# The beginning of a trunk kernel: inputs through two queues, squares in more buffers, the last square summed by its own matmuls, a first power taken early, and low weight halves made by adding transfers

## The chip, the core and the metric

The kernel runs on one core of one Trainium2 chip. A core has engines that run side by side, each with its own instruction stream in order: TensorE (PE, matrix products; its weight loads are shown as PEld), VectorE (DVE, elementwise), ScalarE (ACT, functions of one input), GpSimd (POOL) and SyncE (SP, which issues transfers). Transfers (DMAs) run on 16 DMA engines that all issuing queues share. The metric is the device time in microseconds, the median over runs.

## The reference

A trunk of two layers on 512 positions of width 1024: one layer with a gated linear recurrence (HGRN2), one with chunked band attention, each with a gated FFN behind it. The change lies in the first sub-layer, of which this is the part that matters:

```python
c_act = jax.nn.silu(c)
sm = jax.nn.softmax(a_lb.astype(jnp.float32), axis=0)
lower_bounds = jnp.cumsum(sm, axis=0) - sm[0]
...
mod = c_act @ mod_w[layer] + mod_b[layer]
sh1, sc1, g1, sh2, sc2, g2 = jnp.split(mod, N_MOD, axis=-1)
u = modulate(rms_norm(h, norm_mix[layer]), sh1, sc1)
...
q, z_f, v, g = jnp.split(u @ w_in, [A_FORGET_DIM, 2 * A_FORGET_DIM, 2 * A_FORGET_DIM + D_MODEL], axis=-1)
q = jax.nn.silu(q)
sig = jax.nn.sigmoid(zf)
f = lbf + (1 - lbf) * sig
```

`rms_norm(x, gain)` is `x * rsqrt(mean(x * x) + 1e-6) * gain`, and `modulate(x, shift, scale)` is `x * (1 + scale) + shift`. `v` are the values of the recurrence; `lbf` are the lower bounds of its forget gate.

## The kernel before

Everything is kept transposed: a tile is 128 features (partitions) by 512 positions, and eight tiles `h[0]` to `h[7]` hold the residual stream. Products are made in three passes, because PE takes the operands in a rounded 32-bit format (F32R): each operand is split into a high part (a rounded copy, made by ACT) and a low part (the difference, made by DVE), and `mm3` (L180) adds high x high, high x low and low x high. A weight block of 128 x 1024 is loaded into a buffer `raw` (three of them), `split` (L120) makes `wh` on ACT (L123) and `wl` on DVE (L128). For one pair of FFN blocks per layer, which `by_transfer` (L116) names, `wl` is made in another way: ACT writes the negated rounded copy (L125) and POOL issues a transfer that adds `raw` to it (L126). `fetch` (L147) splits one block ahead of its use, and one more where the next is by transfer.

The start runs in this order:

- SP loads `cols` (all column vectors), `ident`, the eight `h`, and then in turn rows of the modulation matrix (`mrow`, 512 KB) and first weight blocks (`fall`, `first_r`, 384 KB).
- ACT loads the table of its sigmoid and makes `csig`; DVE makes `cact` = silu(c), and eight scaled identities `dc` from it, which PE multiplies by ones (L955) to spread `cact` over all partitions; ACT copies that to `crow`. ACT also loads the table of Exp for the lower bounds (L99 to L108).
- The mean square: ACT squares each `h[j]` (L223, L227, two buffers), DVE adds the squares up in `acc` (L230), PE sums over partitions with four one-column matmuls (`mean_square`, L235). `rstd` (L238) adds epsilon on ACT (L242) and raises to -0.5 on POOL (L244), which is the first power in the kernel. `bcast` (L247) makes four scaled identities `dg` on DVE and spreads them by PE into `rb`.
- For each j, `mod_entry` (L615) makes one column of the modulation by a 128 x 1024 multiply and sum on DVE (L618), `prepare` (L633) makes the modulated tile `u_t` (L641), its high part `u00h` on ACT (L645) and its low part `u00l` on DVE (L648), and `low` (L630) the low part of the first weights; `first_mm` (L662) then runs 18 products into six banks. The sixth and seventh tile take the shift too (`shifted`, L655), and their parts are called `u0h` and `u0l` (L658, L659); the other six get theirs behind the first products, in `complete`.
- Between those, PE runs matmuls whose results are never read (L959 and L967, into `first[0]`, which the first product overwrites); they keep PE occupied.
- Next come the values, `value_half(0)`: four blocks `av_0_0` to `av_0_3`, each used by 24 matmuls (L206 to L208). Around them `evacuate` copies the six banks (L1002) and `shift_sums` (L993, L995) sums shift products, which PE sums once more at L1025. The gates follow, from L686, and need `lb` and `oml` at L702 to L707.

The order in this stretch is written out by hand (`tc.manual_schedule()`); behind it, a scheduler orders what the generators yield. All engines work in order: an instruction that waits holds up everything behind it on its engine, and SP's loads, which wait for free buffers, do so too.

## Time and profile before

| | us |
|---|---|
| median of 3 runs | 1282.65 |
| the runs | 1279.99, 1282.65, 1286.14 |
| the profiled execution | 1283.68 |
| its span, first to last instruction | 1281.5 |
| first product that counts starts at | 19.09 |
| values' products start at | 53.67 |

A row of the timeline has the start, the duration, the engine, the line, the operation and the tiles (out<-in); numbers of buffers are left out, so `av_l` is any `av_0_k_l`. In brackets stands how long the engine sat idle before, and what ended that. A row of a table of waits has the total, the count and the longest, in us. PE's matmuls are pipelined, so two in sequence may overlap in the rows.

### The profile page before, as it was taken

To read this page: it belongs to the slowest core of one execution; us is meant where nothing else is said; L and a number is where in the kernel's file an instruction comes from. 1 tells how busy PE (TensorE), PEld (TensorE's weight loads), DVE (VectorE), ACT (ScalarE), POOL (GpSimd) and SP (SyncE) were. 2 spreads that over 40 slices of the span, in tenths; PEclk is the share of its full clock that TensorE was granted. 3 is DMA by queue.
4 is the path that set the end of the run, shared out by engine and by line. 5 is a ranking of instruction groups with operands and counts; after the bars stand their busy time and mean duration, and the time that the engine had idled before them with its cause. 6 is when DMAs were issued, how large, how long until landed. Compare 5 with 4: busy or idle time off the path is not lost.

```text
span 1281.5 us, 21575 instructions
## 1 busy us (share of the span) xinstructions
PE 1255.6 (98%) x8544; PEld 1070.2 (84%) x8544; DVE 990.7 (77%) x1812; ACT 637.7 (50%) x1119; POOL 20.8 (2%) x28
## 2 busy tenths in 40 slices
PE   7999999999999999999999999999999999999996
PEld 6878778788899999978888766676889999998886
DVE  7998888946999999986359656776798888884324
ACT  4464436443655565642228456674465556563220
POOL 0000000000000000000000000000000000000000
PEclk9999999999999999999999999999999999999999
DMA  9456666522455655666342322211333333342321
GB/s 367 166 181 194 224 223 207 193 80 85 109 203 182 197 185 195 209 204 204 91 130 82 107 74 73 79 58 34 115 91 107 104 114 113 100 124 91 94 88 66
DMA packets 53333, 177.55 MB, mean 139 GB/s; under 512 B 6000, under 2 KB 9456, under 8 KB 53232
## 3 DMA queue, kind: packets, MB, share of 16 engines
q1 hardware_dynamic: 52656, 174.08, 41.3%
q0 software_dynamic: 576, 2.10, 1.0%
q8 instruction: 67, 1.10, 0.4%
q14 instruction: 34, 0.28, 0.1%
HBM read 171.96 MB, written 2.10 MB: 136 GB/s over the span
## 4 chain that ended last, share of the span: by engine, by line
PE 81%; DVE 12%; DMA 3%; issue 2%; ACT 1%; POOL 1%; SPq 0%; POOLq 0%; DVEq 0%; ACTq 0%
PE f_r L532 8%; PE f_r L533 8%; PE f_r L531 7%; PE f_o L185 6%; PE f_o L183 6%; PE f_o L184 6%; DVE mw L315 2%; DMA mw<-in_modw 2%; PE t L1183 2%; PE f L183 2%; PE f L184 2%; PE f L185 2%; PE s L1166 2%; DVE f_w_l L497 1%; PE bo L1197 1%
## 5 line engine op out<-in xcount | busy, mean ns | idle before, releaser
L532 PE MATMUL f_r<-f_l,f_w_h 128*128 128x256 f32 x1008 | 287.0, 285 | 0.0
L533 PE MATMUL f_r<-f_h,f_w_l 128*128 128x256 f32 x1008 | 282.1, 280 | 0.9 <-DVE f_w_l L497 0.8
L531 PE MATMUL f_r<-f_h,f_w_h 128*128 128x256 f32 x1008 | 280.7, 279 | 0.0
L533 PEld LDWEIGHTS f_r<-f_h,f_w_l 128*128 128x128 f32 x1008 | 189.0, 188 | 2.1 <-DVE f_w_l L497 1.9
L531 PEld LDWEIGHTS f_r<-f_h,f_w_h 128*128 128x128 f32 x1008 | 189.5, 188 | 0.3 <-ACT f_pu L553 0.2
L532 PEld LDWEIGHTS f_r<-f_l,f_w_h 128*128 128x128 f32 x1008 | 189.5, 188 | 0.1
L185 PE MATMUL f_o<-f_p,f_o_l 128*128 128x512 f32 (+1 forms) x374 | 141.6, 380 | 0.5 <-DVE f_o_l L128 0.5
L183 PE MATMUL f_o<-f_p,f_o_h 128*128 128x512 f32 (+1 forms) x374 | 141.9, 380 | 0.0
L184 PE MATMUL f_o<-f_p,f_o_h 128*128 128x512 f32 (+1 forms) x374 | 140.9, 377 | 0.2 <-DVE f_p L448 0.2
L315 DVE SCALAR_TENSOR_TENSOR mw<-mw,crow 128x1024 f32<-128x1024 f32 x96 | 116.8, 1221 | 17.5 <-DMA mw<-in_modw 17.3
L123 ACT ACTIVATE f_o_h<-r_f_o 128x1024 fp32r<-128x1024 f32 (+1 forms) x48 | 46.8, 987 | 137.8 <-PE f_o L184 116.6
L128 DVE TENSOR_TENSOR f_o_l<-r_f_o,f_o_h 128x1024 fp32r<-128x1024 f32 (+1 forms) x48 | 54.0, 1134 | 69.0 <-ACT f_o_h L123 62.4
L496 ACT ACTIVATE f_w_h<-f_x 128x1024 fp32r<-128x1024 f32 x72 | 76.5, 1062 | 49.3 <-PE f_r L532 40.6
L497 DVE TENSOR_TENSOR f_w_l<-f_x,f_w_h 128x1024 fp32r<-128x1024 f32 x72 | 88.0, 1223 | 5.7 <-ACT f_w_h L496 3.2
L496 ACT ACTIVATE f_w_h<-r_f_c 128x1024 fp32r<-128x1024 f32 x72 | 61.0, 847 | 49.0 <-PE f_r L532 47.4
L185 PEld LDWEIGHTS f_o<-f_p,f_o_l 128*128 128x128 f32 x374 | 70.1, 188 | 15.8 <-DVE f_o_l L128 1.9
L184 PEld LDWEIGHTS f_o<-f_p,f_o_h 128*128 128x128 f32 x374 | 70.2, 188 | 14.5 <-DVE f_p L448 0.7
L183 PEld LDWEIGHTS f_o<-f_p,f_o_h 128*128 128x128 f32 x374 | 70.3, 188 | 12.5
L497 DVE TENSOR_TENSOR f_w_l<-r_f_c,f_w_h 128x1024 fp32r<-128x1024 f32 x72 | 68.8, 955 | 10.1 <-ACT f_w_h L496 10.1
L1172 ACT ACTIVATE sb<-sb,st 128x128 f32<-128x128 f32 (+1 forms) x64 | 35.6, 557 | 41.5 <-DVE st L1171 41.3
L1169 DVE CUSTOM_DVE_ANT_0 sb<-s,wb 128x128 f32<-128x128 f32 (+1 forms) x64 | 31.0, 490 | 29.5 <-PE s L1166 29.2
L184 PE MATMUL f<-f_l,f_h 128*128 128x512 f32 x96 | 37.4, 396 | 0.0
(381 smaller groups left out, 2724.2 us busy)
## 6 DMA issues: line engine op xcount, KB each, us to landing
mw<-in_modw SPq DMA_DIRECT2D x96, 512.0 KB, 4.1
r_f_c<-in_ffn_in SPq DMA_DIRECT2D x72, 512.0 KB, 3.4
r_f_o<-in_ffn_out SPq DMA_DIRECT2D x32, 512.0 KB, 3.7
mrow<-in_modw SPq DMA_DIRECT2D x16, 512.0 KB, 8.7
r_f<-in_ffn_in SPq DMA_DIRECT2D x16, 512.0 KB, 3.3
r_f_o<-in_ffn_out SPq DMA_DIRECT2D x16, 384.0 KB, 3.3
r_av<-in_a_v SPq DMA_DIRECT2D x8, 512.0 KB, 3.7
r_g<-in_a_g SPq DMA_DIRECT2D x8, 512.0 KB, 4.5
```

Source lines behind the costliest of these rows:

```text
L123: A.activation(wh, raw, AF.Copy)
L128: V.tensor_sub(wl, raw, wh)
L183: T.matmul(ps, wh[:, kt, :], uh, start=start, stop=False)
L184: T.matmul(ps, wh[:, kt, :], ul, start=False, stop=False)
L185: T.matmul(ps, wl[:, kt, :], uh, start=False, stop=stop)
L315: V.scalar_tensor_tensor(mw, mw, 1.0, crow, op0=ALU.mult, op1=ALU.mult, accum_out=raw[:, j:j + 1])
L496: A.activation(wh, raw, AF.Copy)
L497: V.tensor_sub(wl, raw, wh)
L531: T.matmul(ps, wh[:, j, :], uh, start=f, stop=False, skip_group_check=True)
L532: T.matmul(ps, wh[:, j, :], ul, start=False, stop=False, skip_group_check=True)
L533: T.matmul(ps, wl[:, j, :], uh, start=False, stop=stop and j == 3, skip_group_check=True)
L1172: A.activation(s[:, 0:n], s[:, 0:n], AF.Exp, bias=st[:, 1:2], accum_out=st[:, 2:3])
```

## The change

- `cols`, `ident`, `h3` and `h5` are loaded by transfers that ACT issues; SP issues the other six `h`.
- POOL takes a power of ones early, into `pow0`, which nothing reads.
- The lower bounds move into `bounds()`, called behind the third group of the values' products.
- The low parts of all four blocks of the first half of the values are made by an adding transfer.
- PE's filler matmuls on `h[j]` as they land become three on `h[0]` before the sums, three after and three after the broadcast.
- The squares take three kinds of buffer in turn, two of each; DVE no longer adds the last one to `acc`, and PE sums it with four matmuls of its own, into four more columns. The two copies of `crow` move from ACT into DVE's additions. Epsilon and the two sums are added on DVE.

```diff
--- before.py
+++ after.py
@@ -54,7 +54,7 @@
 V1_AFTER, CREDIT, RATES = 1, 3.0, (3.5, 16, 2.0, 56, 1.5)
 
 
-KEEP = 3
+IDLE = (3, 3, 3)
 
 
 EARLY = (3, 5)
@@ -78,12 +78,13 @@
 
 
     cols = cst.tile([P, NCOL], F32, tag="cols", name="cols")
-    nc.sync.dma_start(cols, d["cols"])
+    A.dma_start(cols, d["cols"])
     ident = cst.tile([P, P], F32, tag="ident", name="ident")
-    nc.sync.dma_start(ident, d["ident"])
+    A.dma_start(ident, d["ident"])
+
     h = [cst.tile([P, S], F32, tag=f"h{j}", name=f"h{j}") for j in range(KT)]
     for j in range(KT):
-        nc.sync.dma_start(h[j], d["xT"][j * P:(j + 1) * P, :])
+        (A if j in (3, 5) else nc.sync).dma_start(h[j], d["xT"][j * P:(j + 1) * P, :])
 
     ones = cst.tile([P, P], F32, tag="ones", name="ones")
     V.memset(ones, 1.0)
@@ -93,19 +94,23 @@
     V.memset(eps, EPS)
     nhalf = cst.tile([P, 8], F32, tag="nhalf", name="nhalf")
     V.memset(nhalf, -0.5)
-
+    pow0 = sm.tile([P, NB], F32, tag="rs", name="pow0")
+    G.tensor_tensor(pow0, ones[:, 0:NB], nhalf[:, 0:NB], op=ALU.pow)
     lb = cst.tile([P, AH], F32, tag="lb", name="lb")
     oml = cst.tile([P, AH], F32, tag="oml", name="oml")
-    lbt = sm.tile([P, AH], F32, tag="lbt", name="lbt")
-    V.tensor_sub(lbt, cols[:, C_LB:C_LB + AH], cols[:, C_LB:C_LB + AH])
-    lbe = sm.tile([P, AH], F32, tag="lbe", name="lbe")
-    A.activation(lbe, lbt, AF.Exp)
-    lbr = sm.tile([P, AH], F32, tag="lbr", name="lbr")
-    V.reciprocal(lbr, lbe)
-    lbs = sm.tile([P, AH], F32, tag="lbs", name="lbs")
-    V.tensor_mul(lbs, lbe, lbr)
-    V.tensor_sub(lb, lbs, lbs)
-    V.tensor_scalar(oml, lb, -1.0, 1.0, op0=ALU.mult, op1=ALU.add)
+
+    def bounds():
+
+        lbt = sm.tile([P, AH], F32, tag="lbt", name="lbt")
+        V.tensor_sub(lbt, cols[:, C_LB:C_LB + AH], cols[:, C_LB:C_LB + AH])
+        lbe = sm.tile([P, AH], F32, tag="lbe", name="lbe")
+        A.activation(lbe, lbt, AF.Exp)
+        lbr = sm.tile([P, AH], F32, tag="lbr", name="lbr")
+        V.reciprocal(lbr, lbe)
+        lbs = sm.tile([P, AH], F32, tag="lbs", name="lbs")
+        V.tensor_mul(lbs, lbe, lbr)
+        V.tensor_sub(lb, lbs, lbs)
+        V.tensor_scalar(oml, lb, -1.0, 1.0, op0=ALU.mult, op1=ALU.add)
 
     cact = cst.tile([P, KT], F32, tag="cact", name="cact")
     csig = sm.tile([P, KT], F32, tag="csig", name="csig")
@@ -115,7 +120,7 @@
 
     def by_transfer(key):
 
-        return key[0] in [f"f{layer}" for layer in FAST] and key[1] == PLAIN - 1
+        return key[0] in [f"f{layer}" for layer in FAST] and key[1] == PLAIN - 1 or key[0] == "av" and key[1] == 0
 
     def split(raw, nk, n, nm, tag, key):
         wh = wp.tile([P, nk, n], F32R, tag=tag + "h", name=f"{nm}_h")
@@ -946,6 +951,11 @@
             load_first(j)
         load_mod(0, 0)
 
+        def idle(n):
+
+            for _ in range(n):
+                T.matmul(first[0][:, 0:256], ones, h[0][:, 0:256], start=True, stop=True)
+
         pcs = []
         for r in range(2):
             dc = hp.tile([P, NB, P], F32, tag=f"on{6 + r}", name=f"dc{r}")
@@ -955,19 +965,35 @@
                 T.matmul(pcs[r][:, k * P:(k + 1) * P], ones, dc[:, k, :], start=True, stop=True)
         gb = cst.tile([P, KT], F32, tag="gb", name="gb")
         V.scalar_tensor_tensor(gb, cols[:, C_MB + 8:C_MB + 16], 1.0, cols[:, C_NM:C_NM + KT], op0=ALU.add, op1=ALU.mult)
+        idle(IDLE[0])
+
+        sqs = []
         for j in range(KT):
-            T.matmul(first[0][:, 0:256], ones, h[j][:, 0:256], start=True, stop=True)
-            square_into(acc, j, "n0")
-        for r in range(2):
-            A.activation(crow[:, r * S:(r + 1) * S], pcs[r], AF.Copy)
-        pst = mean_square(acc, "n0")
+            sq = sm.tile([P, S], F32, tag=("sq", "et", "ut")[j % 3], name=f"n0_sq{j}", bufs=2) if j else acc
+            A.activation(sq, h[j], AF.Square)
+            sqs.append(sq)
+            if 0 < j < KT - 1:
+                V.tensor_add(acc, acc, sq)
+            if j == 3:
+                V.tensor_copy(crow[:, 0:S], pcs[0])
+            elif j == 5:
+                V.tensor_copy(crow[:, S:D], pcs[1])
+        pst = bank("n0_ss")
+        for i, sq in enumerate((acc, sqs[-1])):
+            for b in range(NB):
+                T.matmul(pst[:, NB * i + b:NB * i + b + 1], sq[:, b * P:(b + 1) * P], mean_col, start=True, stop=True)
         a0 = mod_entry(0, 1)
         high(0)
-        for _ in range(KEEP):
-            T.matmul(first[0][:, 0:256], ones, h[0][:, 0:256], start=True, stop=True)
-        rs = rstd(pst, "n0")
+        idle(IDLE[1])
+        ms = sm.tile([P, NB], F32, tag="ms", name="n0_ms")
+        V.tensor_scalar_add(ms, pst[:, 0:NB], EPS)
+        ms2 = sm.tile([P, NB], F32, tag="ms", name="n0_ms2")
+        V.tensor_add(ms2, pst[:, NB:2 * NB], ms)
+        rs = sm.tile([P, NB], F32, tag="rs", name="n0_rs")
+        G.tensor_tensor(rs, ms2, nhalf[:, 0:NB], op=ALU.pow)
         low(0)
         rb = bcast(rs, "n0")
+        idle(IDLE[2])
         prepare(0, a0)
         for j in range(KT):
             if j + 1 < KT:
@@ -1010,6 +1036,8 @@
             evacuate(i)
         for k in range(KT):
             push(4 * k + 1)
+            if k == 2:
+                bounds()
             if k == 0:
                 evacuate(4)
                 evacuate(5)
```

The start on ACT (`csig` is the sigmoid of c, `n0_sq` the squares, `first0_h` the first weights' high part). Before:

```order
L112 ACT_TABLE_LOAD
L112 ACTIVATE csig_108<-cols_67 128x8
L102 ACT_TABLE_LOAD
L102 ACTIVATE lbe_99<-lbt_97 128x8
L223 ACTIVATE acc0_118<-h0_71 128x512
L227 ACTIVATE n0_sq1_0_196<-h1_72 128x512
```

ACT's first rows now:

```order
L81 DMA cols_67<-in_cols 128x177
L83 DMA ident_69<-in_ident 128x128
L87 DMA h3_74<-in_xT 128x512
L87 DMA h5_76<-in_xT 128x512
L117 ACT_TABLE_LOAD
L117 ACTIVATE csig_100<-cols_67 128x8
L973 ACTIVATE acc0_110<-h0_71 128x512
```

Four transfers stand ahead of the first table load, and the second table load with `lbe` has left this place.

PE at the same place (`n0_ss` are the sums over partitions, `n0_rb0` is the broadcast, `first0<-h` are fillers). Before:

```order
L959 MATMUL first0_119<-h5_76,ones_87 128x256
L959 MATMUL first0_119<-h6_77,ones_87 128x256
L959 MATMUL first0_119<-h7_78,ones_87 128x256
L235 MATMUL n0_ss0_225<-mean_89,acc0_118 128x1 x4
L967 MATMUL first0_119<-h0_71,ones_87 128x256 x3
L254 MATMUL n0_rb0_246<-n0_dg0_245,ones_87 128x128 x4
```

And now:

```order
L957 MATMUL first0_111<-h0_71,ones_87 128x256 x3
L984 MATMUL n0_ss_211<-mean_89,acc0_110 128x1 x4
L984 MATMUL n0_ss_211<-mean_89,n0_sq7_209 128x1 x4
L957 MATMUL first0_111<-h0_71,ones_87 128x256 x3
L259 MATMUL n0_rb0_238<-n0_dg0_237,ones_87 128x128 x4
L957 MATMUL first0_111<-h0_71,ones_87 128x256 x3
L188 MATMUL first0_111<-u00h0_252,first0_h_224 128x512
```

The sums are eight matmuls instead of four, and three fillers stand between the broadcast and the first product.

The second place is the step from the first products to the values. ACT before (`u0h` are high parts of the modulated tiles, `f0` and `qq0` take the first products' banks):

```order
L658 ACTIVATE u0h7_479<-u0_t7_472,a0_7_476 128x512
L658 ACTIVATE u0h0_514<-u0_t0_255,a0_0_504 128x512
L123 ACTIVATE av_0_0_h_522<-r_av_0_0_311 128x1024
L658 ACTIVATE u0h1_548<-u0_t1_268,a0_1_512 128x512
L1002 ACTIVATE f0_507<-first0_119 128x512
L1002 ACTIVATE qq0_506<-first1_120 128x512
```

ACT now:

```order
L663 ACTIVATE u0h7_474<-u0_t7_467,a0_7_471 128x512
L663 ACTIVATE u0h0_509<-u0_t0_250,a0_0_499 128x512
L128 ACTIVATE av_0_0_h_517<-r_av_0_0_306 128x1024
L130 ACTIVATE av_0_0_l_518<-r_av_0_0_306 128x1024
L128 ACTIVATE av_0_1_h_522<-r_av_0_1_513 128x1024
L130 ACTIVATE av_0_1_l_523<-r_av_0_1_513 128x1024
L663 ACTIVATE u0h1_549<-u0_t1_263,a0_1_507 128x512
L1028 ACTIVATE f0_502<-first0_111 128x512
```

Three operations on weights have come in between the first block's high part and `u0h1`.

PE there, with what each row waits for (a name that begins with DMASW is the landing of a transfer issued by POOL). Before:

```order
L185 MATMUL first4_123<-u0h7_479,first7_l_470 128x512
L183 MATMUL first5_124<-u0h7_479,first7_h_469 128x512
L184 MATMUL first5_124<-u0l7_480,first7_h_469 128x512
L185 MATMUL first5_124<-u0h7_479,first7_l_470 128x512
L206 MATMUL av_0_0_556<-av_0_0_h_522,u0h0_514 128x512 [waits Activation_49]
L207 MATMUL av_0_0_556<-av_0_0_l_523,u0h0_514 128x512 [waits DVE_49]
L208 MATMUL av_0_0_556<-av_0_0_h_522,u0l0_515 128x512
```

And now:

```order
L190 MATMUL first5_116<-u0h7_474,first7_l_465 128x512
L211 MATMUL av_0_0_557<-av_0_0_h_517,u0h0_509 128x512 [waits Activation_49]
L212 MATMUL av_0_0_557<-av_0_0_l_518,u0h0_509 128x512 [waits DMASW0_49]
L213 MATMUL av_0_0_557<-av_0_0_h_517,u0l0_510 128x512 [waits DVE_49]
L211 MATMUL av_0_1_558<-av_0_0_h_517,u0h0_509 128x512 [waits PE_49]
```

The order of PE is the same; its second matmul of the values now waits for the transfer instead of for DVE. Behind this stretch, the rows of DVE and SP differ by places of one or two, since the scheduler sets them anew.

## The prediction

> **What bounds the kernel now.** I read the page's busy times and its chain of waits first, then the table of what TensorE (PE) waited for, and then the timeline, engine by engine, up to 85 us.
>
> ```profile
> span 1281.5 us, 21575 instructions
> ...
> PE 1255.6 (98%) x8544; PEld 1070.2 (84%) x8544; DVE 990.7 (77%) x1812; ACT 637.7 (50%) x1119; POOL 20.8 (2%) x28
> ...
> PE 81%; DVE 12%; DMA 3%; issue 2%; ACT 1%; POOL 1%; SPq 0%; POOLq 0%; DVEq 0%; ACTq 0%
> ```
>
> PE is busy for 1255.6 of 1281.5 us, and the change removes no matmul that computes a product. It can only let PE start its real work earlier, or make it wait later. Where PE waits:
>
> ```profile
> PE crow L955 <- DVE dc L954: 3.5, 1, 3.5
> ...
> PE first L183 <- ACT u00h L645: 1.5, 1, 1.5
> ...
> PE av L208 <- DVE u0l L659: 0.5, 1, 0.5
> ...
> PE fine L757 <- DVE ks L733: 2.4, 4, 0.8
> PE ot L850 <- DVE oe L841: 1.6, 1, 1.6
> ```
>
> The columns are total, times and longest, in us. The first two lie in the first 19 us. The third is the only wait between 23 and 130 us. The last two, with 1.2 us of smaller ones, make 5.2 us between 130 and 260 us. So the start is a chain that ends at the first product, and from there PE hardly stops. What counts is when that chain ends, and whether PE still finds every operand behind it.
>
> The chain in rows of the timeline (start, duration, engine, line, tiles):
>
> ```profile
> 0.73 1.28 ACT L112 ACT_TABLE_LOAD   x1 [0.73 <-PEq L1442]
> ...
> 1.66 3.75 SPq L86 DMA_DIRECT2D h<-in_xT  x8
> 2.74 0.21 ACT L112 ACTIVATE csig<-cols 128x8 f32<-128x8 f32 x1 [0.72 <-DMA cols<-in_cols]
> ...
> 3.18 1.46 DVE L954 TENSOR_SCALAR dc<-ident,cact 128x128 f32<-128x128 f32 x7
> ...
> 6.22 0.69 DVE L230 TENSOR_TENSOR acc<-acc,n_sq 128x512 f32<-128x512 f32 x1 [0.83 <-ACT n_sq L227]
> ...
> 8.07 4.67 DVE L230 TENSOR_TENSOR acc<-acc,n_sq 128x512 f32<-128x512 f32 x6 [1.16 <-ACT n_sq L227]
> ...
> 12.80 1.05 PE L235 MATMUL n_ss<-mean,acc 128*128 128x1 f32 x8 [1.15 <-DVE acc L230]
> ...
> 14.23 1.82 POOL L244 TENSOR_TENSOR n_rs<-n_ms,nhalf 128x4 f32<-128x4 f32 x1 [13.19 <-ACT n_ms L242]
> ...
> 16.09 0.88 DVE L253 TENSOR_SCALAR n_dg<-ident,n_rs 128x128 f32<-128x128 f32 x4 [0.91 <-POOL n_rs L244]
> ...
> 19.09 0.69 PE L183 MATMUL first<-u00h,first_h 128*128 128x512 f32 x1 [1.50 <-ACT u00h L645]
> ...
> 23.05 0.39 PE L183 MATMUL first<-u00h,first_h 128*128 128x512 f32 x1
> ```
>
> The reader is to see seven dependent additions on DVE that end at 12.74, the sums over partitions on PE, one power of 1.82 us on POOL, and the first product at 19.09.
>
> **The start.** *Loads issued by ACT.* SP issues one load in about 0.46 us (eight in 3.75 us). At that price four take 1.9 us on ACT: the table load moves from 0.73 to 2.6, csig from 2.74 to 3.9, and the eight dc (0.21 us apart) end near 6.1. The trace has no load issued by ACT. If they cost nothing csig stays where it is; at twice SP's price it comes 3 us late. I take SP's price, the same instruction on another queue. SP's own later loads move up by those four issues. *Additions.* The first then stands at 6.2, as before. The second waited 1.16 us for its square, which waited for a load. The first load of h is now issued at 0.73 instead of 1.66 and squares have buffers enough, so I let the additions follow each other 0.80 us apart (six in 4.67 us).
>
> ```profile
> L244 POOL TENSOR_TENSOR n_rs<-n_ms,nhalf x6: 695/1008/1817, 14.2 to 1273.1; 128x4 f32<-128x4 f32 x4, 128x2 f32<-128x2 f32 x2
> ...
> L1190 DVE COPY pt<-t 128x384 f32<-128x384 f32 x16 | 8.9, 555 | 1.2 <-PE t L1183 0.8
> ```
>
> The two copies of crow come from ACT to DVE. One of 384 columns takes 0.56 us, so one of 512 about 0.7; between two dependent additions it also fills their 0.1 us pause and lengthens the row by some 0.45. Six additions and two copies end at 6.2 + 5 x 0.80 + 2 x 0.45 + 0.7 = 11.8, against 12.74. *Sums.* Leaving the last square out of the chain saves an addition but costs four matmuls, eight more PE entries at 1.05 us for eight: PE is through at 11.86 + 2.05 = 13.9, where it was through at 13.85. Two small DVE operations (0.17 us for 128x8 ones, the nearest) replace ACT's bias; the power starts at 14.4, 0.2 us late. *Power.* 1.82 us is the longest of six, the median is 1.0. With pow0 paying the first cost while POOL idles, 0.8 us goes, and the dg start at 15.46 instead of 16.09. **DVE's chain is 0.6 us earlier**; between 0 (the power still costs 1.8) and 1.6 (ACT issues for nothing).
>
> *Fillers.* After its gaps PE ran at half clock:
>
> ```profile
> 15.00:20.00 5.00, 2.29 (x12) 1.34 (x11) 2.74 (x8) 1.36 (x2) 1.05 (x1) 0.92 1.03 417
> 20.00:25.00 5.00, 5.00 (x17) 4.01 (x18) 4.86 (x10) 1.37 (x2) 0.00 (x0) 0.74 1.03 418
> ```
>
> The third column from the right is the granted clock: 0.92 and 0.74 make 3.4 us at half speed, in which eight products came 0.43 us apart and not 0.23, a loss of 1.6 us. Three times three fillers now leave gaps of 2 us at most, so I expect full speed at the first product; if the clock drops all the same, little changes, because PE cannot use most of that gain. DVE feeds it, and at the last of the first products PE has nearly caught up with DVE:
>
> ```profile
> 48.69 0.74 DVE L659 SCALAR_TENSOR_TENSOR u0l<-u_t,a,u0h 128x512 fp32r<-128x512 f32 x1
> ...
> 49.82 0.39 PE L184 MATMUL first<-u0l,first_h 128*128 128x512 f32 x1
> ```
>
> u0l is ready at 49.43 and used at 49.82. With DVE 0.6 earlier PE gets it at 48.8: **PE ends the first products 1.0 us earlier** (0.6 + 0.4), at 52.7 instead of 53.67.
>
> **The values' low parts.** Before, ACT makes the high part, DVE subtracts, and PE uses the result at once:
>
> ```profile
> 50.80 0.73 ACT L658 ACTIVATE u0h<-u_t,a 128x512 fp32r<-128x512 f32 x1 [2.18 <-DVE a L623]
> ...
> 51.44 1.04 ACT L123 ACTIVATE av_h<-r_av 128x1024 fp32r<-128x1024 f32 x1
> ...
> 52.38 0.71 ACT L658 ACTIVATE u0h<-u_t,a 128x512 fp32r<-128x512 f32 x1
> ...
> 52.69 1.22 DVE L128 TENSOR_TENSOR av_l<-r_av,av_h 128x1024 fp32r<-128x1024 f32 x1
> ...
> 53.96 0.50 PE L207 MATMUL av<-av_l,u0h 128*128 128x512 f32 x1
> ...
> 65.88 0.50 PE L208 MATMUL av<-av_h,u0l 128*128 128x512 f32 x1 [0.50 <-DVE u0l L659]
> ```
>
> The subtraction ends at 53.9, its reader runs at 53.96: there is no slack. After, ACT writes a second copy and POOL issues a transfer that adds to it. The same pair stands in this trace for one ffn block:
>
> ```profile
> 344.18 1.04 ACT L125 ACTIVATE f_l<-r_f 128x1024 fp32r<-128x1024 f32 x1
> ...
> 345.54 0.86 POOL L126 DMA_DIRECT2D f_l<-r_f  x1 [2.44 <-ACT f_l L125]
> ...
> L126 POOL DMA_DIRECT2D f_l<-r_f x4: 862/892/1047, 342.0 to 955.6; - x4
> ...
> DMA to landing us min/median/max: 4.6/5.0/5.5
> ```
>
> 1.04 us of ACT, 0.3 us to POOL's start, 5.0 us to the landing. There it is hidden, since that block is split one piece ahead. Here the first piece's copy stands directly behind the high part on ACT: it runs from 52.38 - 0.6 to 52.8, the transfer starts at 53.1 and lands at 58.1. PE's second matmul of the values, due at 53.0, waits 5.1 us, and everything on PE stands behind it. The bounds for the landing are 3.5 us (the page's plain load of r_av, the same 512 KB) and 8.7 us (its mrow, loaded while the queues were full); I take the median of the operation itself. The other three pieces are needed some 5.5 us apart and land in time. ACT's u0h of the next block now stands behind three more weight operations, but PE waits longer than they take. Each raw buffer is held until its transfer has read it, so SP issues the fourth r_av at 58 instead of 53.93, landing near 62; ACT needs it at 65.
>
> *Clock.* The half-speed spell followed gaps of 1.17 and 1.5 us; a stop of 5 us should bring it again, for 1.6 us as above. The Trainium skill, page "TensorE: Matmul & The Clock Gate", section "What's actually happening", says that the clock falls after at least one idle window of about 3.4 us and that windows run freely; read strictly, a 5 us stop need not hold a whole idle window, and the sum would be 1.6 us lower. This trace disagrees: shorter gaps were enough.
>
> *DVE and bounds.* DVE loses four subtractions (4.9 us). Five small operations of bounds, the Exp and its table load (1.28 us) move to about 67 us. There lbe stands on ACT behind the fourth piece's two copies, whose buffer PE frees late, and u0l stands behind it on DVE: I expect PE to wait about 0.6 us there, as much as the wait at 65.88 that goes. DVE's lighter load may take a little of the later 5.2 us of waits; I count 0.5.
>
> **Sum.** The profiled execution took 1283.68 us for its span of 1281.5; it lies 1.03 above the median of 1282.65. -1.0 (start) + 5.1 (stop) + 1.6 (clock) - 0.5 (later) = +5.2: 1288.9 on that execution, **1288 us** on the median.
>
> **Rivals.** *Slow landing* (the other side, clearly slower): at 50 to 55 us the DMA engines are 85% busy, and the transfer reads two operands.
>
> ```profile
> 50.00:55.00 5.00, 5.00 (x23) 3.88 (x22) 4.93 (x10) 4.20 (x8) 0.00 (x0) 1.00 0.85 308
> ```
>
> At a landing of 6.5 us or with a second half-clock spell the loss is 5.2 + 1.5 to 3 = +7 to +8.5: 1290 to 1291.5. It decides from a landing of 6.2 us on. Against it: the four in the trace also ran beside loads. *Absorbed*: DVE's 4.9 us let PE skip the waits between 130 and 260 us, +0 to +2: 1283 to 1285. For it speaks that DVE ends the longest of them; against it that what feeds DVE there (first_b, the scores) comes from PE, and is late with it. *No half clock*, as the page read strictly: 1286.3. *The stop doesn't come* (the change does as its words say, and the low parts are in time): start -1.0 to -2, and the wait of 0.5 goes: 1280 to 1281.5. It needs a landing in under 1 us, against 4.6 at least.
>
> **Chances.** Forecast (1287 to 1289.5) 0.40; slow landing 0.25; no half clock 0.15; absorbed 0.13; no stop 0.07. A measurement of this kernel tells about 0.5% from no change, 6.4 us: slower needs over 1289.1, which takes the slow landing and a sixth of the forecast, 0.31; faster needs under 1276.2, which no case gives, 0.03 for what I have not seen; the rest 0.66. The range 1281.5 to 1292 leaves out the last case and the end of the slow one.
>
> **What would show it.** Right: the dg of the first norm near 15.5, its power near 1.0 us; PE's first product near 18.4 at clock 1.00; "PE av <- DMA" as the longest wait, about 5 us near 53; clock under 0.85 between 55 and 65. Wrong: no such wait; a first product later than 19.1 (ACT's issues dearer than taken); or the waits between 130 and 260 us gone.

## The result and the profile after

The changed kernel takes 1293.01 us (median of four runs, 1291.54 to 1294.31) against 1283.28 for the kernel before (median of four runs, the three above among them): ratio 1.0076, 95% interval 1.0048 to 1.0105. It is slower by about 10 us, where 5.2 were forecast. Its profiled execution took 1294.11 us, with a span of 1292.3.

The page of the changed kernel, busy times and the shares of the chain that ended last:

```profile
span 1292.3 us, 21598 instructions
...
PE 1260.0 (98%) x8548; PEld 1072.3 (83%) x8548; DVE 986.8 (76%) x1811; ACT 639.4 (49%) x1120; POOL 25.5 (2%) x33
...
PE 74%; DVE 13%; DMA 6%; issue 4%; ACT 3%; POOL 0%; DVEq 0%; SPq 0%; POOLq 0%; ACTq 0%
```

DMA's share of the chain has doubled. The same kernel's table of what PE waited for (total, times, longest):

```profile
PE crow L965 <- DVE dc L964: 5.2, 1, 5.2
PE av L212 <- DMA av_l<-r_av: 4.8, 1, 4.8
PE fine L762 <- DVE ks L738: 3.8, 4, 1.8
...
PE ot L855 <- DVE oe L846: 1.3, 1, 1.3
...
PE av L213 <- DVE u0l L664: 0.6, 1, 0.6
```

The second row is new and is the stop that the prediction described; the wait for `ks` has grown from 2.4 to 3.8. The beginning in the timeline of the changed kernel:

```profile
3.92 0.21 ACT L117 ACTIVATE csig<-cols 128x8 f32<-128x8 f32 x1
...
4.81 1.66 DVE L964 TENSOR_SCALAR dc<-ident,cact 128x128 f32<-128x128 f32 x8 [0.49 <-DMA ident<-in_ident]
...
8.23 1.49 DVE L976 TENSOR_TENSOR acc<-acc,n_sq 128x512 f32<-128x512 f32 x2 [1.08 <-ACT n_sq L973]
...
12.23 0.68 DVE L976 TENSOR_TENSOR acc<-acc,n_sq 128x512 f32<-128x512 f32 x1
...
13.88 1.18 PE L984 MATMUL n_ss<-mean,n_sq 128*128 128x1 f32 x8
...
15.37 0.96 DVE L636 TENSOR_TENSOR first_l<-fall,first_h 128x768 fp32r<-128x768 f32 x1
15.53 1.67 POOL L993 TENSOR_TENSOR n_rs<-n_ms,nhalf 128x4 f32<-128x4 f32 x1 [13.41 <-DVE n_ms L991]
...
20.44 0.49 PE L188 MATMUL first<-u00h,first_h 128*128 128x512 f32 x1 [0.20 <-ACT u00h L650]
```

The additions end at 12.91 instead of 12.74 (11.8 was forecast), the power still takes 1.67 us, and the first product comes 1.35 us later than before. Around the stop the timeline has:

```profile
52.62 1.05 ACT L128 ACTIVATE av_h<-r_av 128x1024 fp32r<-128x1024 f32 x1
...
53.58 1.04 ACT L130 ACTIVATE av_l<-r_av 128x1024 fp32r<-128x1024 f32 x1
...
54.94 1.05 POOL L131 DMA_DIRECT2D av_l<-r_av  x1 [16.76 <-ACT av_l L130]
...
59.92 0.79 PE L212 MATMUL av<-av_l,u0h 128*128 128x512 f32 x1 [4.83 <-DMA av_l<-r_av]
```

The transfer lands 4.9 us after POOL starts on it, and PE reads it at 59.92. The span's extra 10.8 us can be cut at three events of PE: the first product of the values (54.70 against 53.67), the first product with a low part (59.92 against 53.96), and the first of `zf` behind the values (86.64 against 77.85). That gives **+1.0** for the beginning, **+4.9** for the stop, **+2.8** between the stop and `zf`, and **+2.0** for all that follows. The forecast had -1.0, +5.1, +1.6 and -0.5, so the beginning came out 2.0 us dearer, the clock 1.2 and the rest 2.5, while the stop came out right.

### The profile page after: what moved, and what is told of

Read it like the earlier page. It is cut to its first block, busy times and chain, and to the rows that moved or that the text cites. A ratio compares the mean times of both kernels' runs of the same rounds, so it can differ in the third digit from the quotient of the medians.

```text
span 1292.3 us, 21598 instructions
## 1 busy us (share of the span) xinstructions
PE 1260.0 (98%) x8548; PEld 1072.3 (83%) x8548; DVE 986.8 (76%) x1811; ACT 639.4 (49%) x1120; POOL 25.5 (2%) x33
## 4 chain that ended last, share of the span: by engine, by line
PE 74%; DVE 13%; DMA 6%; issue 4%; ACT 3%; POOL 0%; DVEq 0%; SPq 0%; POOLq 0%; ACTq 0%
PE f_r L537 6%; PE f_r L538 6%; PE f_r L536 6%; PE f_o L190 6%; PE f_o L189 6%; PE f_o L188 6%; DVE f_w_l L502 3%; DVE mw L320 3%; DMA mw<-in_modw 3%; DMA r_f_c<-in_ffn_in 2%; PE t L1211 2%; PE s L1194 2%; PE bo L1225 1%; PE bq L188 1%; PE f L188 1%
```

## The experiments

The same cuts for every profiled execution, in us, with the time against the kernel before on the same chip. The cuts are of one execution each, the ratios of medians:

| kernel | first product | values start | stop | to zf | zf to end | ratio, 95% interval |
|---|---|---|---|---|---|---|
| before | 19.09 | 53.67 | 0.29 | 23.89 | 1203.7 | 1 |
| changed | 20.44 | 54.70 | 5.22 | 26.72 | 1205.7 | 1.0076 (1.0048 to 1.0105) |
| changed, again (r1) | 21.17 | 55.59 | 5.04 | 25.44 | 1206.6 | 1.0082 (1.0063 to 1.0100) |
| e1 transfers alone | 18.45 | 53.39 | 4.30 | 24.59 | 1203.9 | 1.0053 (1.0038 to 1.0067) |
| e2 beginning alone | 20.04 | 54.30 | 0.45 | 25.03 | 1202.7 | 1.0027 (1.0016 to 1.0039) |
| e3 later pieces | 19.75 | 54.16 | 0.45 | 25.83 | 1204.4 | 1.0034 (1.0021 to 1.0048) |
| e4 busy stop | 19.85 | 54.12 | 5.14 | 23.95 | 1203.5 | 1.0047 (1.0033 to 1.0060) |
| u1 loads on SP | 20.66 | 54.90 | 0.47 | 25.02 | 1202.8 | 1.0018 (1.0009 to 1.0028) |
| u2 last in chain | 19.56 | 53.78 | 0.50 | 25.03 | 1203.1 | 1.0015 (1.0005 to 1.0025) |
| u4 crow on ACT | 19.99 | 53.34 | 0.30 | 25.06 | 1201.2 | 0.9999 (0.9990 to 1.0008) |
| p1 first_l later | 21.21 | 55.63 | 0.49 | 25.03 | 1203.0 | 1.0015 (1.0005 to 1.0025) |
| c1 crow on DVE | 20.36 | 55.70 | 0.22 | 23.06 | 1201.6 | 1.0006 (0.9996 to 1.0015) |
| b1 bounds later | 19.38 | 54.26 | 0.23 | 24.84 | 1203.3 | 1.0013 (1.0005 to 1.0022) |
| v1 first_l later | 19.08 | 53.94 | 0.23 | 23.71 | 1202.4 | 0.9999 (0.9990 to 1.0008) |
| v2 best beginning | 18.24 | 53.14 | 0.23 | 23.66 | 1203.2 | 0.9993 (0.9985 to 1.0002) |
| w1 issued earlier | 21.91 | 56.34 | 0.96 | 26.12 | 1205.4 | 1.0054 (1.0042 to 1.0066) |
| w2 both | 18.84 | 53.71 | 1.40 | 24.07 | 1206.9 | 1.0014 (1.0001 to 1.0026) |

"Stop" runs from the values' first product to the first with a low part, "to zf" from there to the first product of `zf`. e1, c1, b1 and v1 start from the kernel before, v2 from v1, w2 from v2, e2, e3, e4 and w1 from the changed kernel, and u1, u2, u4 and p1 from e2.

### The two halves of the change

e1, on the kernel before:

```diff
-        return key[0] in [f"f{layer}" for layer in FAST] and key[1] == PLAIN - 1
+        return key[0] in [f"f{layer}" for layer in FAST] and key[1] == PLAIN - 1 or key[0] == "av" and key[1] == 0
```

> The kernel before with one part of the change alone: the low parts of the first values by adding transfers. Theory (the stop and the half-speed clock behind it are most of the loss, the new beginning costs about 1 us): first products end at 53.7 us as before, TensorE waits 4.5 to 5.5 us for the first adding transfer, two windows at half clock follow and cost 2.5 to 3 us, the time is 7.5 to 9 us over the kernel before (ratio about 1.006). Rival (the prediction's sum: stop 5.1, clock 1.6, less 0.5): 6 to 6.5 us over. Rival (the beginning is what costs): under 5 us over.

Measured: 1290.63 us, 6.8 over before (0.0053 x 1283.5), with a wait of 3.9 us:

```profile
PE av L207 <- DMA av_l<-r_av: 3.9, 1, 3.9
```

The 6.8 are below the theory's range and inside neither rival's, but the interval, 4.9 to 8.6, reaches into all three. The forecast of two windows at half clock failed: only one followed, for a reason shown below.

e2 takes the same edit back in the changed kernel:

```diff
-        return key[0] in [f"f{layer}" for layer in FAST] and key[1] == PLAIN - 1 or key[0] == "av" and key[1] == 0
+        return key[0] in [f"f{layer}" for layer in FAST] and key[1] == PLAIN - 1
```

> The changed kernel with the values' low parts by DVE again, so that only the new beginning is left. Theory: the first products end about 1 us later than before (54.7 instead of 53.7), no wait for an adding transfer, granted clock 1.0 from 50 to 66 us, time +0.5 to +2 us against the kernel before. Rival (the prediction's term for the start): -1 us. Rival (the beginning costs more than its start shows, through the clock or the later waits): over +3 us.

Measured: 1287.53 us, 3.5 over (2.1 to 5.0). That is above the theory's range and in the last rival's. So the beginning costs, where it was to gain 1.0. The two halves add up to 10.3, about what the whole loses. In part this is chance: e2's time to `zf` holds 1.1 us more than before's (25.03 against 23.89), which a kernel with the transfers and no half clock does not show (e4: 23.95). The trace of e2 shows less than its median: its execution took 1284.68 us, the second fastest of 12 (1283.16 to 1289.74).

e3 keeps the transfers for the pieces behind the first:

```diff
-        return key[0] in [f"f{layer}" for layer in FAST] and key[1] == PLAIN - 1 or key[0] == "av" and key[1] == 0
+        return key[0] in [f"f{layer}" for layer in FAST] and key[1] == PLAIN - 1 or key[0] == "av" and key[1] == 0 and key[2] > 0
```

> The changed kernel with transfers only for the second, third and fourth piece of the first values; DVE makes the first one's low part. Theory (only the first transfer stands in TensorE's way): no wait of over 1 us for an adding transfer, no half clock between 50 and 70 us, time within 0.7 us of the kernel with the new beginning alone. Rival (DVE's freed 3.6 us are worth something): 1 to 3 us faster than that. Rival (the second transfer is late as well, since its raw block is held): a wait of 2 to 5 us near 60 us and 3 to 8 us slower than that.

Measured: 1286.86 us, no wait over 0.7 us there, clock 1.00 from 50 to 70 us; the same as e2 within the intervals. Only the first piece's transfer stands in PE's way, and three subtractions off DVE (3.7 us) buy nothing.

### The clock behind the stop

e4 has PE repeat a product while it waits:

```diff
             wh, wl = weight(key + (kp,))
+            if key == ("av", 0) and kp == 0:
+                for _ in range(20):
+                    T.matmul(pss[0], u[0][0][:, 0:P], wh[:, 0, :], start=True, stop=True)
```

> The changed kernel with the first product of the values repeated 20 times before it is used, so that TensorE works through its stop. Theory (the stop's idle time lets the clock fall, and the fall costs 2.7 us): the first low product still starts near 59.9, granted clock 1.0 from 55 to 70 us, time 2.3 to 3 us under the changed kernel. Rival (the clock falls for another reason, or its fall costs nothing because DVE feeds TensorE there): within 1 us of the changed kernel.

Measured: 1289.91 us, 3.1 under the changed kernel by the medians and 3.7 by the ratios; the low product comes as late (a stop of 5.14), the stretch to `zf` is 23.95 instead of 26.72. So the theory held. r1 is the changed kernel unaltered.

> The changed kernel once more, for a second profile. Theory (the clock is set per window of 3.41 us whose phase differs between executions, so a stop of the same length costs one or two of them): stop of 4 to 5.5 us again, and one or two half-speed windows behind it, 0.7 to 3 us; the beginning's additions end between 12.0 and 13.0 with the landing of the third load of h. Rival (always two windows): 6.8 us at half clock again.

Measured: 1294.04 us, the stop again (4.6 us of waiting), and one window at half clock, not two. The tables below cut the time where the clock changed; from left: the stretch, its length, PE's busy time, then the other engines, the granted clock, DMA's share, GB/s. The changed kernel:

```profile
55.58:58.99 3.41, 0.00 (x0) 0.00 (x0) 1.84 (x3) 3.41 (x7) 1.29 (x2) 1.00 0.94 210
58.99:62.40 3.41, 2.48 (x6) 1.99 (x7) 0.22 (x3) 3.41 (x6) 0.87 (x1) 0.50 0.98 185
62.40:65.82 3.42, 3.42 (x10) 2.65 (x9) 3.22 (x7) 0.74 (x2) 0.00 (x0) 0.50 0.85 231
65.82:69.23 3.41, 3.41 (x17) 2.80 (x16) 1.03 (x3) 0.96 (x1) 0.00 (x0) 1.00 1.05 271
```

Its second execution, r1:

```profile
57.04:60.45 3.41, 0.00 (x0) 0.00 (x0) 2.06 (x4) 3.41 (x7) 0.87 (x1) 1.00 0.93 177
60.45:63.87 3.42, 3.24 (x8) 2.56 (x9) 0.38 (x1) 3.42 (x6) 0.87 (x1) 0.50 1.02 216
63.87:67.28 3.41, 3.41 (x17) 2.80 (x16) 3.38 (x7) 0.19 (x1) 0.00 (x0) 1.00 0.95 276
```

And e1:

```profile
54.49:57.91 3.42, 0.22 (x1) 0.23 (x2) 2.05 (x4) 3.42 (x8) 0.86 (x1) 1.00 1.03 194
57.91:61.33 3.42, 3.42 (x9) 2.64 (x9) 0.76 (x2) 3.23 (x6) 0.86 (x1) 0.50 1.05 235
```

e4, whose repeated product fills the stop:

```profile
55.38:58.80 3.42, 3.42 (x17) 2.69 (x15) 2.06 (x4) 3.42 (x7) 0.90 (x2) 1.00 0.89 166
58.80:62.21 3.41, 3.19 (x15) 2.45 (x14) 0.23 (x1) 3.41 (x6) 0.87 (x1) 1.00 1.02 216
```

In these traces the clock changes only at the ends of stretches of 3.41 us, whose phase differs from execution to execution. An idle one is followed by one at half speed. In the changed kernel that one began 0.93 us before the stop ended, so it was busy for 2.48 us only and a second followed; in r1 it was busy for 3.24 us, and the clock came back. By the same cuts, "to zf" was 26.72, 25.44 and, without a spell but else alike (e4), 23.95: two half-speed stretches cost 2.8 us, one 1.5. In e1 the one cost 0.7 more than before's 23.89.

The Trainium skill, page "TensorE: Matmul & The Clock Gate", section "What's actually happening", says that the windows run freely, that the clock falls after an idle one and rises after a busy one. The two executions of the changed kernel agree; e1's window held 0.22 us of work, and the clock fell behind it too.

### What the beginning lost

u1, u2, u4 and p1 each take one part of the beginning back or alter it, in e2.

```diff
 u1
-    A.dma_start(cols, d["cols"])
+    nc.sync.dma_start(cols, d["cols"])
...
-        (A if j in (3, 5) else nc.sync).dma_start(h[j], d["xT"][j * P:(j + 1) * P, :])
+        nc.sync.dma_start(h[j], d["xT"][j * P:(j + 1) * P, :])
 u2
-            if 0 < j < KT - 1:
+            if 0 < j:
                 V.tensor_add(acc, acc, sq)
-        for i, sq in enumerate((acc, sqs[-1])):
+        for i, sq in enumerate((acc,)):
...
 u4
-            if j == 3:
-                V.tensor_copy(crow[:, 0:S], pcs[0])
-            elif j == 5:
-                V.tensor_copy(crow[:, S:D], pcs[1])
+        for r in range(2):
+            A.activation(crow[:, r * S:(r + 1) * S], pcs[r], AF.Copy)
 p1
-        low(0)
         rb = bcast(rs, "n0")
+        low(0)
```

> The new beginning alone, with all loads issued by SP again. Theory (the four issues on ACT hold the first dc up by 0.9 to 1.7 us, but the additions behind it make up most, since they wait for the squares): first dc at 3.2 to 4.0 us instead of 4.8 to 5.0, first addition near 6.1 instead of 6.5, first product 0.3 to 0.5 us earlier than the 19.75 to 20.0 of the new beginning. Rival (the loads of h spread over two queues land earlier than from one): the additions from the third on come later and the first product is not earlier. The time itself moves by less than a measurement tells.

Measured: dc starts at 3.17, the additions at 6.10 instead of 6.52, and they end at 11.58, 0.5 earlier than in e3 and e4, whose loads landed early too. But the sums then took 11.63 to 15.21 at half clock, and the first product came at 20.66, later. The theory's price of ACT's issues holds up to the additions' end; what they are worth at the first product stays open.

> The new beginning alone, with the last square added on DVE again, so that one row of four sums is made. Theory (apart it costs as much as it gains): additions end 0.7 to 0.8 us later, from their end to the power's start 1.5 to 1.8 us instead of 2.5, first product within 0.3 us. Rival (the prediction's reading, the same cost): 0.2 us earlier power start. Rival (the second row of sums is the loss): power start 0.3 to 1 us earlier.

Measured: additions end at 12.86 (e3 and e4: 12.03 and 12.11), the power starts at 14.41 (14.51 and 14.59), the first product at 19.56 (19.75 and 19.85). As the theory had it, summing the last square apart buys nothing.

> The new beginning alone, with the two copies of crow on ACT behind the squares again. Theory (the copies of 0.68 us stand inside DVE's chain of additions, which is not waiting for loads then): additions end 0.7 to 1.4 us earlier, power start and first product 0.6 to 1.2 us earlier. Rival (the chain waits for the squares of the last loads, so the copies cost nothing): no change over 0.2 us.

Measured: additions end at 11.40, the power starts at 13.87, 1.0 earlier than in e2 and 0.6 to 0.7 earlier than in e3 and e4, whose second square came early as it does here. The first product does not gain: PE spread `rb` at half clock from 15.91 to 17.99. The time is 3.6 us under e2's (0.9999 against 1.0027), of which the trace shows 1.0 at the values' start.

> The new beginning alone, with DVE's subtraction for the first weights' low part (first_l, 0.96 us) behind the four dg instead of beside POOL's power. Theory (POOL stands still while DVE runs this subtraction of two operands in SBUF; the power took 1.01 + 0.83 x its overlap with it in three kernels): power 1.0 us instead of 1.67, dg 0.65 us earlier, first product 0.5 to 0.65 us earlier. Rival (the power's time depends on its values, ones being quick): power 1.65 us all the same, first product later by up to 0.5 us.

Measured: the power takes 1.01 us. The timeline of p1:

```profile
12.17 1.47 PE L984 MATMUL n_ss<-mean,acc 128*128 128x1 f32 x8 [1.65 <-DVE acc L976]
...
13.51 1.84 PE L984 MATMUL n_ss<-mean,n_sq 128*128 128x1 f32 x8
...
15.83 1.01 POOL L993 TENSOR_TENSOR n_rs<-n_ms,nhalf 128x4 f32<-128x4 f32 x1 [13.71 <-DVE n_ms L991]
...
17.66 0.95 DVE L636 TENSOR_TENSOR first_l<-fall,first_h 128x768 fp32r<-128x768 f32 x1
```

So the extra time was neither the first use nor the values. In the kernel before, `first_l` began together with the power, whose row the prediction shows, and the power took 1.82:

```profile
14.23 0.95 DVE L631 TENSOR_TENSOR first_l<-fall,first_h 128x768 fp32r<-128x768 f32 x1
```

Here 0.95 us lay beside it; in the changed kernel 0.80 us of it lay beside the power, which took 1.67; with none beside it, 1.01. `pow0`, early and on ones, took 1.01 too and changed nothing. So POOL stands still for most of the time that DVE's subtraction runs beside it. The Trainium skill, page "SBUF — State Buffer", section "SBUF: two separate sides", has this rule: DVE and GpSimd share a pair of ports, held for a whole instruction by whichever starts first, also by a DVE operation with two SBUF inputs against a GpSimd operation that reads SBUF. The three durations agree (0.81 for 0.95 beside it, 0.66 for 0.80).

The theory's earlier first product did not come: it starts at 21.21. That is the clock again: p1's two rows of sums took 1.5 and 1.8 us where e2's took 1.05 and 1.03.

Then two parts alone, put into the kernel before: c1 the copies of `crow` as in the change, b1 the bounds (the lines that move them into `bounds()` are those of the change).

```diff
 c1
             square_into(acc, j, "n0")
-        for r in range(2):
-            A.activation(crow[:, r * S:(r + 1) * S], pcs[r], AF.Copy)
+            if j == 3:
+                V.tensor_copy(crow[:, 0:S], pcs[0])
+            elif j == 5:
+                V.tensor_copy(crow[:, S:D], pcs[1])
 b1
...
             push(4 * k + 1)
+            if k == 2:
+                bounds()
```

> The kernel before with one part of the change alone: the two copies of crow by DVE between the additions. Theory (they lengthen DVE's chain by 0.4 us each where it is not waiting for squares): additions end 0.8 us later against the same start and landings (about 12.8 us where the second square is not late), first product 0.5 to 0.8 us later than 18.45, time +0.5 to +2 us. Rival (these copies carry most of the beginning's 3.5 us, as their removal from the new beginning gained 4): +3 to +4 us. Rival (they cost nothing): within 0.3 us.

Measured: additions end at 13.27 although the second one started 0.28 earlier than before, so 0.8 later for the two copies; time 1284.11, +0.8 us with an interval that holds 0. The copies are not most of the beginning's loss; u4's gain of 3.6 is not explained by them alone.

> The kernel before with one part of the change alone: the bounds' five small operations and Exp moved behind the third block of the values. Theory (DVE sets the pace there until 66 us, and the operations take 1.2 us of it): TensorE's wait for u0l near 66 us is 1.5 us instead of 0.5, zf starts 1.0 us later than in the kernel before, time +0.5 to +1.5 us. Rival (the beginning gains as much, since DVE and ACT are relieved there): no change. Rival (the prediction's reading): 0.6 us of wait.

Measured: 1284.51, +1.7 us (0.6 to 2.8). DVE's timeline in b1, then PE's wait:

```profile
64.08 0.16 DVE L102 TENSOR_TENSOR lbt<-cols 128x8 f32<-128x8 f32 x1
64.52 0.20 DVE L106 RECIPROCAL lbr<-lbe 128x8 f32<-128x8 f32 x1 [0.28 <-ACT lbe L104]
...
65.16 0.17 DVE L110 TENSOR_SCALAR oml<-lb 128x8 f32<-128x8 f32 x1
65.24 1.22 DVE L620 SCALAR_TENSOR_TENSOR mrow<-mrow,crow 128x1024 f32<-128x1024 f32 x1
```

```profile
PE av L210 <- DVE u0l L661: 1.5, 1, 1.5
```

The small operations hold DVE for 1.16 us just where it sets PE's pace, as the theory had it. All kernels with the bounds there and no transfers need 24.84 to 25.06 to `zf`, those without 23.06 to 23.89. Together c1 and b1 measure 2.5 us of e2's 3.5; but u4, which keeps the bounds, measures none, so the parts do not simply add, and what carries the rest stays open. With all four transfers and no half clock the bounds cost nothing that can be seen (e4: 23.95); DVE then has four subtractions less.

### Better versions

v1 is the kernel before with p1's edit; v2 has besides more buffers for the squares, the last square summed apart and epsilon added on DVE, all as in the change, with loads, crow, fillers and bounds as before.

```diff
 v2, on v1
+            sq = sm.tile([P, S], F32, tag=("sq", "et", "ut")[j % 3], name=f"n0_sq{j}", bufs=2) if j else acc
+            A.activation(sq, h[j], AF.Square)
+            sqs.append(sq)
+            if 0 < j < KT - 1:
+                V.tensor_add(acc, acc, sq)
...
```

> The kernel before with DVE's first_l behind the four dg, so that it doesn't run beside POOL's power. Theory (POOL stands still beside this subtraction): power 1.0 us instead of 1.6 to 1.8, dg 0.6 to 0.8 us earlier, first product 0.3 to 0.8 us earlier, time -0.3 to -1 us, which a measurement hardly tells. Rival (first_l then stands before the first u and gives it back): power 1.0 us, first product within 0.2 us of before.

> The kernel before with first_l behind the dg, more buffers for the squares and the last square summed apart; loads on SP, crow on ACT and the fillers as before. Theory: additions end at 10.9 to 11.5 us, power starts by 13.8 and takes 1.0, first product at 17.6 to 18.2 us, time -0.5 to -2 us, faster than the kernel before if anything here is. Rival (a second half-speed window falls on the sums, as it did in two runs of the new beginning): sums over 3 us, first product after 18.4, no gain.

Measured: v1 1282.45, v2 1282.10. In v2 the chain reads:

```profile
14.07 1.01 POOL L981 TENSOR_TENSOR n_rs<-n_ms,nhalf 128x4 f32<-128x4 f32 x1 [13.04 <-DVE n_ms L979]
...
18.24 0.49 PE L183 MATMUL first<-u00h,first_h 128*128 128x512 f32 x1 [1.61 <-ACT u00h L645]
```

The power is 1.01 in both. v1 gives the gain back (PE spreads `rb` at half clock, 15.66 to 17.58), v2 keeps 0.85 us at the first product and 0.5 at the values' start. v2 is 11 us faster than the changed kernel; against the kernel before, -0.9 us is within what can be measured.

w1 puts the first piece's transfer one block earlier in the changed kernel, w2 does the same with all four transfers on v2:

```diff
         if j:
             high(j)
+        if j == KT - 1:
+            fetch(0, -1)
```

> The changed kernel with the first piece's high part, copy and adding transfer put one block earlier on ACT and POOL (behind the high part of the eighth block's weights); all four transfers stay. Theory (the transfer costs nothing by itself, only because it is issued when TensorE is about to read it): ACT makes the parts at 45 to 48 us, the transfer starts near 48 and lands at 52 to 53.5, TensorE waits under 1 us for it instead of 4.8, no half clock between 50 and 70 us, time 5 to 8 us under the changed kernel, as the new beginning alone (1285 to 1287.5). Rival (the traffic of the transfers or the held raw blocks cost too): no stop, but still 3 us or more over the new beginning alone.

> The best beginning of these runs (loads on SP, crow on ACT, more buffers for the squares, last square apart, first_l behind the dg) with the four adding transfers, the first one block earlier. Theory (behind 53 us TensorE is the bound, so DVE's freed 4.9 us are worth half a microsecond at most): within 1.5 us of the best beginning alone (1282.1 median), 10 to 12 us under the changed kernel. Rival (DVE's relief shortens its stretch up to 66 us and the waits between 130 and 260 us): 2 to 4 us faster than the best beginning alone. Rival (later transfers come late): a wait of 1 to 4 us at the second or fourth piece.

Measured: w1 1290.81, w2 1284.89. The stop shrank and the half clock behind it was gone, as forecast, but neither time was: w1 is 3.2 us under the changed kernel (r1) and 3.3 over e2, near its rival's case, and w2 is 2.8 over v2. PE's waits and POOL's issue in w1:

```profile
PE av L212 <- DMA av_l<-r_av: 2.3, 2, 1.7
```

```profile
49.38 1.05 POOL L131 DMA_DIRECT2D av_l<-r_av  x1 [11.47 <-DVE u_t L648]
```

The stop shrinks to 0.96 and 1.40. But PE reads the first low part at 57.30, so this transfer took 7.9 us (7.2 in w2) instead of 4.7 to 4.9. While it was under way SP issued further loads of `r_av` and `mrow`, in the changed kernel none; DVE was also busy for 7.66 of the 7.87 us there and for 2.37 of 4.94 in the changed kernel. The changed kernel's third piece speaks for the loads: it took 9.7 us, with three of SP's loads around it and DVE busy for 4.25. In w1 a later piece is late by 1.7. Another part of w1's distance from its expectation is its beginning, whose sums ran at half clock (12.80 to 16.14), so that the values start 1.6 later than in the changed kernel. And the kernels with transfers lose something else. "zf to end" is 1201.2 to 1203.7 in the ten executions without them (mean 1202.7) and 1203.5 to 1206.9 in the seven with them (1205.2); the medians of e3 and e2 do not show it. Where the difference is largest, in w2 and r1, it can be followed; DVE and then PE in r1:

```profile
124.77 1.23 DVE L320 SCALAR_TENSOR_TENSOR mw<-mw,crow 128x1024 f32<-128x1024 f32 x1 [2.94 <-DMA mw<-in_modw]
...
130.88 1.23 DVE L320 SCALAR_TENSOR_TENSOR mw<-mw,crow 128x1024 f32<-128x1024 f32 x1 [2.59 <-DMA mw<-in_modw]
...
146.07 1.08 PE L762 MATMUL fine<-qq,ks 128*32 128x32 f32 x64 [3.17 <-DVE ks L738]
```

The same rows in the kernel before:

```profile
115.06 1.23 DVE L315 SCALAR_TENSOR_TENSOR mw<-mw,crow 128x1024 f32<-128x1024 f32 x1 [1.44 <-DMA mw<-in_modw]
...
119.65 1.23 DVE L315 SCALAR_TENSOR_TENSOR mw<-mw,crow 128x1024 f32<-128x1024 f32 x1 [0.93 <-DMA mw<-in_modw]
...
135.33 0.75 PE L757 MATMUL fine<-qq,ks 128*32 128x32 f32 x64 [0.70 <-DVE ks L733]
```

At these two places DVE waits 3.2 us longer for rows of the modulation matrix, everything behind them on DVE is late, and PE waits 3.2 us for `ks` instead of 0.7; the clock is 0.66 in the 5 us behind. r1 and w2 are the only executions with a half-speed stretch near 140 us. Over all of 78 to 260 us DVE's waits for these rows do not tell the kernels apart (7.5 us before, 8.6 in v2, 9.1 in w2, 9.4 in r1).

Why the waits grow there stays open, and there is a rival to the transfers themselves. The scheduler gave all seven executions with transfers one order of DVE's rows behind `zf`, and the ten without them another; SP's loads differ likewise. The second `qq` of that stretch, for one, falls back by five rows, further than the one or two places told above: it now stands behind a multiply of `mw`. Before and after:

```profile
78.22 1.41 DVE L697 SCALAR_TENSOR_TENSOR qq<-qq,fb,sgq 128x512 f32<-128x512 f32 x2
```

```profile
87.72 1.22 DVE L320 SCALAR_TENSOR_TENSOR mw<-mw,crow 128x1024 f32<-128x1024 f32 x1
...
90.32 0.74 DVE L702 SCALAR_TENSOR_TENSOR qq<-qq,fb,sgq 128x512 f32<-128x512 f32 x1
```

No run has the transfers with the old order, or the new order without them.

## Why the prediction was wrong

- **The stop was right**: 5.1 forecast, 4.9 measured, by the price of the same operation elsewhere in the trace. It is nearly half of the loss, and e1 and e3 show that it is the first piece's transfer alone.
- **The start's step failed**: "DVE's chain is 0.6 us earlier" was 1.14 later at the dg (17.23 instead of 16.09). The sums' term was right (2.6 us from the additions' end to the power). For the 1.1 us at the additions' end, the prediction had the ACT issues right up to csig (3.92 for 3.9) but overlooked that `ident` now lands late (dc at 4.81), and "I let the additions follow each other 0.80 us apart" failed at the second, which waited 1.08 us for a square whose load of h was late. In r1 that load was early (additions end at 12.00), and the sums at half clock took the gain instead. "With pow0 paying the first cost" was wrong by 0.67: the power's extra time is DVE's `first_l` beside it (p1, v1).
- **The clock's term was mis-sized**: 1.6 for one spell; 2.8 between the stop and `zf` in the changed kernel, nearly all of it clock (e4 gets 2.77 back), 1.5 in r1. The rival with a second spell (+7 to +8.5) had the second spell, but it came by the phase of the stretches and not by a slow landing. That full speed would hold at the first product was right, but the half-speed stretch moved to the sums and to `rb`, which lie on the path. The rival "no half clock" fell in all three executions with a stop of over 4 us that nothing filled (changed, r1, e1). It stood on a strict reading of the Trainium skill, page "TensorE: Matmul & The Clock Gate", section "What's actually happening"; two of the three stops did hold a whole idle window, and the third fell without one.
- **The later term had the wrong sign**, the largest miss of the four: -0.5 forecast, +2.0 here and +2.5 as a mean over executions. DVE's lighter load took nothing from the waits for `ks`; they grew from 2.4 to 3.8. The prediction put no price on the new order of DVE's and SP's rows behind `zf`; whether that order or the transfers themselves make the waits longer stays open.
- **The bounds** were to cost 0.6 beside a wait of 0.5 that goes, thus nothing: right with the transfers (a wait of 0.6 in the changed kernel), while alone they hold DVE for 1.2 us, and PE waits 1.5 (b1).
- "Absorbed" and "the stop doesn't come" are out. The range ended at 1292, 1 us short: the slow case had a longer stop or a second spell, but kept a start that gained 1.0 and a later stretch that gained 0.5.

## What to carry to other kernels

Taking work off an engine pays only where that engine sets the pace: price the replacement by when its result is first read, which here was 5 us of landing against a subtraction of 1.2 us. The stops of 4 to 5 us here cost their length and one or two half-speed stretches of 3.41 us behind them (0.7 to 2.8 us), and which one was a matter of phase, so give such a term a range up to two stretches. Behind the shorter stops of w1 and w2 (0.96 and 1.40) there was none. A change that moves work between engines can also make the scheduler reorder rows far behind it: compare the orders before the later waits are put down to the change itself. Before an unusually long instruction is called a first use, look at what ran beside it.

## What was not expected of the hardware

- POOL's 128x4 power takes 1.01 us alone and 1.63 to 1.82 beside a DVE subtraction with two inputs in SBUF.
- PE's busy time in the profile does not by itself tell the clock of the next stretch. In u4 a stretch with 3.22 us of busy PE, 1.9 of them sums with one column, is followed by half speed, while r1's with 3.24 us of products is followed by full speed. What counts instead was not tried:

```profile
10.80:14.21 3.41, 3.22 (x23) 2.71 (x22) 2.75 (x7) 1.37 (x3) 0.34 (x1) 1.00 1.03 418
14.21:17.62 3.41, 2.75 (x11) 2.03 (x10) 1.33 (x5) 0.00 (x0) 1.33 (x1) 0.50 1.03 418
```

- The 512 KB adding transfer lands 4.7 to 4.9 us after POOL's start for the first piece in four executions (changed, r1, e1, e4), and 7.2 to 7.9 us when it is issued one block earlier, with plain loads around it. The later pieces took from 4.9 to 9.7 us in the same four; there PE needed them later still.
